# Eight PSUM banks laid out anew, row sums taken from rows without their bias, and a seventh weight slot in a two-layer decoder step

## The chip, the cores and the metric

The kernel runs on one core of a Trainium2 chip. The metric is the device time of one execution in microseconds (us); lower is better. A profiled execution also gives a trace of every instruction on the core's engines: TensorE (PE; PEld is its weight load), VectorE (DVE), ScalarE (ACT), GpSimd (POOL) and SyncE (SP), and of the transfers (DMA).

## The reference

One inference step of a decoder with two layers. Layer 0 mixes tokens by sliding-window attention, layer 1 by gated linear attention; each is followed by a gated FFN with a short convolution, and every sublayer ends in a layer norm. There are 512 prompt rows and 8 sample rows of 1024 features. The change lies in the FFN and in the layer norm ahead of it:

```python
D_MODEL = 1024; SEQ = 512; DEPTH = 2; DEC_BATCH = 8; D_FF = 2816; CONV_W = 3
def conv_ffn(x, buf, w_up, conv_w, conv_b, w_down):
    T = x.shape[1]
    h = x @ w_up
    a, u = h[..., :D_FF], h[..., D_FF:]
    ap = jnp.concatenate([buf.astype(a.dtype), a], axis=1)
    c = conv_b + sum(conv_w[j] * ap[:, j:j + T] for j in range(CONV_W))
    y = (jax.nn.gelu(c, approximate=False) * u) @ w_down
    return y, ap[:, T:]
# in each layer i:
    xp = layer_norm(ALPHA * xp + mp, ln_mix_g[i], ln_mix_b[i])   # mp: the token mixer
    fp, cp = conv_ffn(xp, buf0, ffn_w_up[i], ffn_conv_w[i], ffn_conv_b[i], ffn_w_down[i])
    xp = layer_norm(ALPHA * xp + fp, ln_ffn_g[i], ln_ffn_b[i])
```

The same is done for the sample rows (xs).

## The kernel before

**Numbers.** All operands are float32. Each is split into a high part that TensorE takes whole and a low part, the rest: weights into `wh` and `wl`, rows into `xh` and `xl`. A product is then three matmuls per 128 features: wh·xh, wh·xl and wl·xh. Rows lie transposed (features on the partitions) and in two groups, a with 256 columns and b with 256 and the 8 sample rows.

**Units.** The weights come in *units* of 128 output columns, of 512 KB as a rule. `load_unit` loads a unit on SP's queue into a `raw` tile; ACT makes the high part (L186) and DVE the low part (L192) in one of `WSLOTS` = 6 slots. For some units (`low_by_dma`) the low part is made without DVE: ACT writes the negated high part (L197), and a transfer that POOL issues adds the weights from memory onto it (L198). `run` goes through the units in an order by hand (`order`): a unit's product with group a first, and some units later that with group b; when b is done, the unit's slot is released and the next unit loads (`release`, `load_next`). For the first units of a phase the split is put off (`late`), behind steps of the layer norm that is going on (`parts`).

**The FFN.** There are 22 blocks of 128 gate columns and 128 value columns. Blocks 0 to 3 are *plain*: `ffn_gate` and `ffn_value` each make a `product` into a PSUM bank (`accp`, pool `acc`, four banks); ACT copies the gate out (L764), ACT and DVE do the convolution, ACT the GELU, and DVE multiplies it with the value bank (`hprod`, L785) and splits the result. From block 4 on a block is a *pair* (`ffn_pair`): gate, value and both row groups are made by seven products of half size, with sums of weights and of rows in place of an eighth (Strassen's scheme). One product goes into one bank (`onep`, pool `one`, two banks), six go in twos into tiles of two banks (`widep`, pool `wide`, three tiles). At the first pair the pools of the plain blocks are closed and these take their eight banks. `half_product` writes the matmuls (L292 to L294). The weights of a pair are three slots, made by `pair_tasks`: `upper` (low part by transfer), `lower` and `sums`, and half a slot, `third`. Down products of a finished part of blocks stand between the pairs (`ffn_down2`); those of the last part come at the end (`ffn_down`), the first four (`HEADS`) begun early in `accp` banks and ended when the last block is there.

**Row sums.** The pairs need sums of the two row groups (`th`, `tl`, `t1`). `row_sums` makes them on DVE right after the layer norm. The norm's gain is applied first, its bias only later, by 16 *shifts* on POOL (`shift`, L438: 8 feature blocks, two groups), which stand between the sums, so that each sum finds the bias where it needs it. The sums of the sample rows (`tsum`, L468, L469) need the biased rows; `row_sum1` splits the last sum at the first pair.

**What sets the order.** The code is written in the order of `run`, but a scheduler goes over the program when it is built (`schedule_with_timeline_sim=True`) and sets the order of the instructions on each engine by its own estimate of when each could run; `issue_after` and `keep_in_program_order` bind it in places. On the chip each engine's queue runs in that order. A tile's memory comes from pools, and whatever takes the place of an earlier tile waits for its last reader.

## Time and profile before

| | |
|---|---|
| median of 3 runs | 1149.77 us (1148.25 to 1152.87) |
| the profiled execution's own time | 1149.82 us |
| its span on the core | 1148.1 us |
| PE busy | 1085.6 us, 9174 matmuls |
| DVE busy | 896.0 us |
| ACT busy | 650.6 us |
| POOL busy | 352.7 us |
| mean granted TensorE clock | 0.973 |
| PE waiting for hprod (L785) at the first pair | 15.7 us in two waits, the longer 9.9 |

The span runs from the first to the last instruction on the core, 1.7 us short of the execution's time. Waits are summed by what ended them. In layer 1 of the two (the first) the FFN starts near 175 us and its first pair at 231 us; in the second, near 770 and at 838 us. Times in the trace are counted from the span's start. "Layer 1" and "layer 2" below are these two.

### The profile page before, as it was taken

Reading aid. Unit: us, or ns where it says so; the run is one execution under the profiler, and the core shown is the slowest. Engines: PE = TensorE matmul, PEld = TensorE weight load, DVE = VectorE, ACT = ScalarE, POOL = GpSimd, SP = SyncE. Lnnn points to the kernel's source line nnn. Section 1 sums busy time; section 2 is a strip of 40 time slices with the busy share of each in tenths; the row PEclk is TensorE's granted clock in tenths of the full one; section 3 lists DMA queues with packets and bytes.
Section 4 is the critical chain, followed back from the end, with each engine's and each line's share of the span. In section 5 each row is a group of like instructions: output and inputs, shape, how many; then the busy total and the mean of one; then the engine's idle time right before and its main releaser. Section 6 shows DMA issues by size and latency. Waiting matters only on the chain.

```text
span 1148.1 us, 23839 instructions
## 1 busy us (share of the span) xinstructions
PE 1085.6 (95%) x9174; PEld 1049.6 (91%) x9174; DVE 896.0 (78%) x1784; ACT 650.6 (57%) x1301; POOL 352.7 (31%) x559
## 2 busy tenths in 40 slices
PE   8999997899999999999999999998889999999995
PEld 8897796899999999988899999897789999999985
DVE  7898679758888778868867778789668778777866
ACT  5677555745556665535545556455556665665534
POOL 3575586401111111056311101277411111111045
PEclk9999998989999999999899999998989999999998
DMA  7453023567777777322134454432457777777312
GB/s 235 148 177 97 17 74 102 139 151 179 183 175 177 179 174 181 102 87 92 59 104 138 126 176 157 138 108 95 129 150 180 176 176 182 183 179 179 100 49 75
DMA packets 63601, 158.53 MB, mean 138 GB/s; under 512 B 7896, under 2 KB 28416, under 8 KB 63488
## 3 DMA queue, kind: packets, MB, share of 16 engines
q1 hardware_dynamic: 51536, 119.47, 32.7%
q0 software_dynamic: 9792, 35.66, 18.3%
q10 hardware_dynamic: 2160, 1.89, 0.5%
q8 instruction: 72, 1.18, 0.4%
q14 instruction: 41, 0.34, 0.1%
HBM read 144.32 MB, written 8.47 MB: 133 GB/s over the span
## 4 chain that ended last, share of the span: by engine, by line
PE 63%; DVE 16%; DMA 6%; POOL 5%; ACT 5%; issue 3%; SPq 0%; ACTq 0%; DVEq 0%; POOLq 0%
PE widep L292 8%; PE widep L293 8%; PE widep L294 8%; PE widep L873 5%; PE widep L872 5%; PE widep L871 5%; PE accp L227 4%; PE accp L225 4%; PE accp L229 4%; DMA vb<-dv 2%; PE onep L292 1%; PE onep L294 1%; PE onep L293 1%; DVE wl L192 1%; DMA raw<-in_w_up 1%
## 5 line engine op out<-in xcount | busy, mean ns | idle before, releaser
L297 ACT ACTIVATE wh<-raw 128x1024 fp32r<-128x1024 f32 x72 | 76.4, 1061 | 117.7 <-PE widep L872 84.3
L198 POOL DMA_DIRECT2D wl<-in_w_down x32 | 27.4, 858 | 348.2 <-ACT wl L197 348.2
L186 ACT ACTIVATE wh<-raw 128x1024 fp32r<-128x1024 f32 (+2 forms) x98 | 99.1, 1012 | 59.5 <-PE accp L227 21.6
L293 PE MATMUL widep<-tl,wh 128*128 128x264 f32 (+1 forms) x432 | 119.2, 276 | 0.0
L292 PE MATMUL widep<-th,wh 128*128 128x264 f32 (+1 forms) x432 | 119.2, 276 | 0.0
L294 PE MATMUL widep<-th,wl 128*128 128x264 f32 (+1 forms) x432 | 119.2, 276 | 0.0
L225 PE MATMUL accp<-xs_a,wh 128*128 128x256 f32 x400 | 112.3, 295 | 6.4 <-ACT wh L186 6.0
L225 PE MATMUL accp<-xh_b,wh 128*128 128x264 f32 x400 | 114.4, 286 | 3.1 <-ACT xh_b L423 3.1
L229 PE MATMUL accp<-xh_b,wl 128*128 128x264 f32 x400 | 112.4, 281 | 0.0
L227 PE MATMUL accp<-xl_b,wh 128*128 128x264 f32 x384 | 108.0, 281 | 0.0
L227 PE MATMUL accp<-xs_a,wh 128*128 128x256 f32 x384 | 107.4, 292 | 0.5 <-DVE xs_a L298 0.4
L298 DVE TENSOR_TENSOR wl<-raw,wh 128x1024 fp32r<-128x1024 f32 x72 | 87.9, 1222 | 24.2 <-ACT wh L297 24.2
L192 DVE TENSOR_TENSOR wl<-raw,wh 128x1024 fp32r<-128x1024 f32 (+3 forms) x70 | 82.0, 1178 | 10.6 <-ACT wh L186 9.9
L225 PEld LDWEIGHTS accp<-xs_a,wh 128*128 128x128 f32 x400 | 81.0, 203 | 8.2 <-ACT wh L186 7.0
L809 DVE TENSOR_TENSOR merged<-widep,conv 128x528 f32<-128x528 f32 x72 | 37.4, 560 | 65.4 <-PE widep L294 65.4
L292 PEld LDWEIGHTS widep<-th,wh 128*128 128x128 f32 x432 | 82.3, 190 | 0.0
L294 PEld LDWEIGHTS widep<-th,wl 128*128 128x128 f32 x432 | 82.2, 190 | 0.0
L293 PEld LDWEIGHTS widep<-tl,wh 128*128 128x128 f32 x432 | 82.2, 190 | 0.0
L225 PEld LDWEIGHTS accp<-xh_b,wh 128*128 128x128 f32 x400 | 76.1, 190 | 6.0 <-ACT xh_b L423 3.8
L227 PEld LDWEIGHTS accp<-xs_a,wh 128*128 128x128 f32 x384 | 78.0, 204 | 1.8 <-DVE xs_a L298 1.4
L292 PE MATMUL widep<-xh_b,wh 128*128 128x264 f32 x288 | 79.6, 276 | 0.0
L293 PE MATMUL widep<-xl_b,wh 128*128 128x264 f32 x288 | 79.5, 276 | 0.0
(416 smaller groups left out, 4278.7 us busy)
## 6 DMA issues: line engine op xcount, KB each, us to landing
raw<-in_w_up SPq DMA_DIRECT2D x88, 512.0 KB, 3.6
wl<-in_w_up POOLq DMA_DIRECT2D x36, 512.0 KB, 6.9
raw<-in_w_down SPq DMA_DIRECT2D x32, 512.0 KB, 3.5
wl<-in_w_down POOLq DMA_DIRECT2D x32, 512.0 KB, 6.5
raw<-in_w_gla SPq DMA_DIRECT2D x24, 512.0 KB, 3.5
raw<-in_w_mix_o SPq DMA_DIRECT2D x16, 512.0 KB, 4.3
raw<-in_w_down SPq DMA_DIRECT2D x16, 384.0 KB, 3.1
qs<-hl SPq DMA_DIRECT2D x64, 64.0 KB, 2.2
```

The source lines that it names most:

```text
L186: nc.scalar.activation(h[:, c], r[:, c], AF.Copy)
L192: nc.vector.tensor_tensor(l[:, c], r[:, c], h[:, c].bitcast(F32), op=ALU.subtract)
L225: nc.tensor.matmul(o, h[:, ks], xh, start=k == 0, stop=False)
L227: nc.tensor.matmul(o, h[:, ks], xl, start=False, stop=False)
L229: nc.tensor.matmul(o, l[:, ks], xh, start=False, stop=not tail and k == nt - 1)
L292: self.nc.tensor.matmul(o, h[:, ks], rh, start=k == 0, stop=False)
L293: self.nc.tensor.matmul(o, h[:, ks], rl, start=False, stop=False)
L294: self.nc.tensor.matmul(o, l[:, ks], rh, start=False, stop=k == KD // 2 - 1)
L297: self.nc.scalar.activation(hi, src, AF.Copy)
L298: self.nc.vector.tensor_tensor(lo, src, hi.bitcast(F32), op=ALU.subtract)
L871: nc.tensor.matmul(o, h[:, ks], rh, start=k == 0, stop=False)
L872: nc.tensor.matmul(o, h[:, ks], rl, start=False, stop=False)
```

## The change

There are four edits.

1. *Banks.* `open_wide` opens the pool of single banks ahead of that of two-bank tiles. The single banks are now banks 0 and 1, where the `mps` tiles of the layer norm were; the two-bank tiles are banks 2 to 7.
2. *Row sums.* The sums are taken from rows without the bias, and the bias is added in DVE's own operations (`bias`, and `step`, a difference of biases that POOL makes once). Three DVE operations of 128x1024 become four of 128x256 each. The first subtraction is bound behind `self.rest`, a step of the layer norm, and `row_sums` begins one slot after the norm and not three. All 16 shifts now follow the sums, and `tsum` follows the shifts.
3. *A seventh slot.* When an FFN opens, a slot `extra` is opened for one more unit (pool `wx`), in memory that a conv tile gives up (`nconv_s` shares `sconv`). It takes the seventh unit of the FFN (unit e + 6, where e is its first), is used once and closed; until then a pair's `third` is held back (`half` = 1). The low part of that unit, and of the gate and value units that are loaded without `late`, comes by `low_by_dma`.
4. *Heads.* The four early down products take their banks in the order 2, 3, 0, 1.

```diff
...
         self.psum_cms = cm1, cm0
     def open_wide(self):
-        self.acc, cm0 = self.psum("wide", WIDES)
-        self.one, cm1 = self.psum("one", 2)
+        self.one, cm0 = self.psum("one", 2)
+        self.acc, cm1 = self.psum("wide", WIDES)
         self.psum_cms = cm1, cm0
     def close_psum(self):
...
         if nt == 0:
             return self.load_rank(u)
         r = self.raw.tile([P, KD * P], F32, name="raw")
-        h, l = (self.wts.tile([P, KD * P], F32R, name=name) for name in ("wh", "wl"))
+        h, l = ((self.wx if u == self.extra else self.wts).tile([P, KD * P], F32R, name=name) for name in ("wh", "wl"))
         n = nt * P // pieces
         for c in (slice(i * n, (i + 1) * n) for i in range(pieces)):
             nc.sync.dma_start(out=r[:, c], in_=src[:, c])
             if late:
-                self.spawn(self.parts(u, h[:, c], l[:, c], r[:, c]), 1)
+                self.spawn(self.parts(u, h[:, c], l[:, c], r[:, c], src[:, c]), 1)
                 continue
             if u >= HIACT:
                 nc.scalar.activation(h[:, c], r[:, c], AF.Copy)
             else:
                 nc.gpsimd.tensor_scalar(h[:, c], r[:, c], 1.0, 0.0, op0=ALU.mult, op1=ALU.add)
-            if self.units[u][2] == self.ffn_down2:
+            if self.units[u][2] in (self.ffn_down2, self.ffn_gate, self.ffn_value):
                 self.low_by_dma(l[:, c], h[:, c], src[:, c])
             else:
                 nc.vector.tensor_tensor(l[:, c], r[:, c], h[:, c].bitcast(F32), op=ALU.subtract)
...
         self.nc.scalar.activation(l, h.bitcast(F32), AF.Copy, scale=-1.0)
         self.nc.gpsimd.dma_start(out=l, in_=src, accum_op=ALU.add)
-    def parts(self, u, h, l, r):
+    def parts(self, u, h, l, r, src):
         norm = self.norm if self.norm and self.slot < self.norm[0] else None
...
         n = u - norm[4] if norm else 0
         with behind(norm and (*[norm[1]] * 4, self.square, self.exp)[n]):
             self.nc.scalar.activation(h, r, AF.Copy)
+            if u == self.extra:
+                self.low_by_dma(l, h, src)
+                return
         with behind(norm and (norm[2], *[norm[3]] * 4, self.rest)[n]):
             self.nc.vector.tensor_tensor(l, r, h.bitcast(F32), op=ALU.subtract)
         yield from ()
...
             self.norm = self.slot + HOLD, self.exp, v.ins, xl.ins, self.next_phase() + 1
         if i % 2 == 0:
             if g.i:
-                self.spawn(self.row_sums(i), 3)
+                self.spawn(self.row_sums(i), 1)
             return
         for m in range(KD):
             yield 1 if m else LATEB
...
         nc, half, n = self.nc, KD // 2, P
         a, b = self.groups
-        lo, hi = slice(0, half), slice(half, KD)
+        hi, lo = slice(half, KD), slice(0, half)
         v = nc.vector
-        rows = lambda g, ks: g.x[:, ks, 0:256]
+        bias = lambda m: self.par[:, C_LNB + i * KD + m:C_LNB + i * KD + m + 1]
+        step = self.pp.tile([P, half], F32, name="step")
+        p0 = C_LNB + i * KD
+        nc.gpsimd.tensor_tensor(step, self.par[:, p0 + half:p0 + KD], self.par[:, p0:p0 + half], op=ALU.subtract)
         wide = lambda t: t.rearrange("p (k c) -> p k c", k=half)
         even = lambda t: t.rearrange("p k (j t) -> p k t j", t=2)
+        row = lambda g, k: g.x[:, k, 0:256]
         self.t1 = [self.ln.tile([P, NT - 256], F32, name=name, bufs=c)[:, :256] for name, c in (("sq", 2), ("sq", 2), ("mu", 1), ("msq", 1))]
-        for k in range(half):
-            v.tensor_tensor(self.t1[k], a.x[:, k, 0:256], b.x[:, k, 0:256], op=ALU.subtract)
-            self.shift(b, i, half + k)
+        with self.tc.issue_after(self.rest):
+            v.tensor_tensor(self.t1[0], row(a, 0), row(b, 0), op=ALU.subtract)
+        for k in range(1, half):
+            v.tensor_tensor(self.t1[k], row(a, k), row(b, k), op=ALU.subtract)
         yield 1
         r = wide(self.pp.tile([P, KD * P], F32, name="raw", bufs=2))
         for k in range(half):
-            v.scalar_tensor_tensor(r[:, k], self.t1[k], -1.0, b.x[:, half + k, 0:256], op0=ALU.mult, op1=ALU.subtract)
-            self.shift(a, i, half + k)
-        self.split(self.th[0][:, :, :, :n], self.tl[0][:, :, :, :n], even(r))
-        v.scalar_tensor_tensor(r, r, -1.0, rows(a, hi), op0=ALU.mult, op1=ALU.subtract)
+            v.scalar_tensor_tensor(r[:, k], row(b, half + k), bias(half + k), self.t1[k], op0=ALU.add, op1=ALU.add)
+        th, tl = self.th[0][:, :, :, :n], self.tl[0][:, :, :, :n]
+        nc.scalar.activation(th, even(r), AF.Copy, scale=-1.0)
         for k in range(half):
-            self.shift(b, i, k)
-        yield 1
+            v.scalar_tensor_tensor(tl[:, k], even(r)[:, k], -1.0, th[:, k].bitcast(F32), op0=ALU.mult, op1=ALU.subtract)
+        yield 2
+        for k in range(half):
+            v.scalar_tensor_tensor(r[:, k], r[:, k], bias(half + k), row(a, half + k), op0=ALU.subtract, op1=ALU.subtract)
         self.split(self.th[2], self.tl[2], even(r))
-        v.tensor_tensor(r, rows(b, hi), rows(b, lo), op=ALU.subtract)
+        yield 2
+        for k in range(half):
+            v.scalar_tensor_tensor(r[:, k], row(b, half + k), step[:, k:k + 1], row(b, k), op0=ALU.add, op1=ALU.subtract)
         self.split(self.th[1][:, :, :, :n], self.tl[1][:, :, :, :n], even(r))
+        for m in (*range(half, KD), *range(half)):
+            yield 1
+            for g in (b, a):
+                self.shift(g, i, m)
         ts = self.pp.tile([P, 2, half, NS], F32, name="tsum")
         v.tensor_tensor(ts[:, 0], b.x[:, lo, 256:], b.x[:, hi, 256:], op=ALU.subtract)
         v.tensor_tensor(ts[:, 1], b.x[:, hi, 256:], b.x[:, lo, 256:], op=ALU.subtract)
         for q in range(2):
             self.split(self.th[q][:, :, :, n:], self.tl[q][:, :, :, n:], even(ts[:, q]))
-        yield 1
-        for k in range(half):
-            self.shift(a, i, k)
     def row_sum1(self):
...
         nc.scalar.dma_start(out=self.sconv, in_=self.I["state_conv"][layer])
         self.base = p.tile([P, NF, NS], F32, name="base")
         self.hist = p.tile([P, NF, 2], F32, name="hist")
-        self.nconv_s = p.tile([P, NF, NS, 2], F32, name="nconv_s")
+        self.nconv_s = self.sconv
         self.nconv_p = p.tile([P, NF, 2], F32, name="nconv_p")
         w = lambda j: self.par[:, C_CW + (layer * 3 + j) * NF:C_CW + (layer * 3 + j + 1) * NF].unsqueeze(2).broadcast_to([P, NF, NS])
         b = self.par[:, C_CB + layer * NF:C_CB + (layer + 1) * NF].unsqueeze(2).broadcast_to([P, NF, NS])
...
         end = self.units[u][1] - 1
         if g.i == 0 and m == 0:
-            self.heads = [self.acc.tile([P, 512], F32, name="accp") for _ in range(HEADS)]
+            heads = [self.acc.tile([P, 512], F32, name="accp") for _ in range(HEADS)]
+            self.heads = heads[2:] + heads[:2]
             for i, ps in enumerate(self.heads):
                 self.down_steps(g, u + i, ps, range(end))
         if g.i == 0 and m < HEADS:
...
                 if u == len(self.units):
                     return
                 self.nu += 1
-                late = self.units[u][1] and any(e < u < e + 6 for e in (*self.phases[2:4], *self.phases[5:6]))
+                late = self.units[u][1] and any(e < u < e + 6 + (e != self.phases[3]) for e in (*self.phases[2:4], *self.phases[5:6]))
                 one = [("live", lambda: self.load_unit(u, late=late))]
                 self.todo = self.pair_tasks(u) if self.units[u][2] == self.ffn_pair else one
             kind, f = self.todo[0]
             if kind == "live":
-                if self.live == WSLOTS:
+                if self.more:
+                    self.more, self.extra = False, self.nu - 1
+                elif self.live == WSLOTS:
                     return
-                self.live += 1
+                else:
+                    self.live += 1
             else:
                 if self.half == 1:
                     return
...
         nc = self.nc
         self.plan()
         self.nu = self.live = WSLOTS
-        self.todo, self.half = [], 0
+        self.todo, self.half, self.more, self.extra = [], 0, False, None
         self.attn_open()
         self.later, self.slot, self.seq, self.norm = [], 0, 0, None
         for i, u in self.order():
...
                 self.unit = u
             if i == 0 and pre:
                 pre()
+                if pre != self.gla_open:
+                    self.wx, self.wx_cm = self.open(f"extra{u}")
+                    self.more, self.half = True, 1
+                    self.load_next()
             self.slot += i + 1 if i == 2 else 1
             if i == 2:
                 f(u, *a)
             else:
                 self.resume(f(self.groups[i], u, *a))
-            if i == 1:
+            if i == 1 and u == self.extra:
+                self.close(self.wx_cm)
+                self.half, self.extra = 0, None
+                self.load_next()
+            elif i == 1:
                 self.release()
             self.due()
         while self.later:
```

How the edits stand in the program is shown at three places of the first FFN, as the built programs order them; a row is line, operation, output and inputs, and size, and `x4` counts like instructions in a row. The lines of the program after the change are its own.

POOL, from the layer norm's end to the first pair. Before, the shifts stand in four runs of four between copies of the first plain blocks; the accumulating transfers (L198) come later:

```order
L301 COPY hist<-aext 128x2
L438 TENSOR_SCALAR x_a<-x_a,par 128x256 x4
L438 TENSOR_SCALAR x_b<-x_b,par 128x264 x4
L438 TENSOR_SCALAR x_a<-x_a,par 128x256 x4
L438 TENSOR_SCALAR x_b<-x_b,par 128x264 x4
L761 MEMSET aext 128x2
...
L198 DMA wl<-in_w_up 128x1024
L301 COPY aext<-hist 128x2
L301 COPY nconv_p<-aext 128x2
L301 COPY nconv_s<-aext 128x8
L198 DMA wl<-in_w_down 128x1024
```

After, all 16 stand in one run (8 times the two rows shown in the middle), between the issue for a down unit's low part and that for the low part of a pair's upper weights:

```order
L198 DMA wl<-in_w_up 128x1024
L304 COPY nconv_p<-aext 128x2
L304 COPY sconv<-aext 128x8
L198 DMA wl<-in_w_down 128x1024
L441 TENSOR_SCALAR x_b<-x_b,par 128x264
L441 TENSOR_SCALAR x_a<-x_a,par 128x256
...
L304 COPY aext<-hist 128x2
L198 DMA wl<-in_w_up 128x1024
```

The shifts have moved from ahead of the plain blocks' last products to a place behind one transfer and in front of another; that last one writes `wl_3345`, which is read below.

PE, from the last plain product of group b to the first pair's two-bank tile. Before, the first pair's single-bank product (12 matmuls, `onep_3396`) stands right behind the last plain product, `accp_3332`:

```order
L229 MATMUL accp_3332<-xh_b_89,wl_3091 128x264
L292 MATMUL onep_3396<-xs_a_86,wh_3135 128x256
L293 MATMUL onep_3396<-xs_a_86,wh_3135 128x256
L294 MATMUL onep_3396<-xs_a_86,wl_3136 128x256
...
L292 MATMUL widep_3411<-xs_a_86,wh_3135 128x256
```

After, the first pair's single-bank product (now `onep_3413`) stands earlier, between plain products, and behind the last plain product (`accp_3349`) stands that of the *second* pair, `onep_3606`:

```order
L232 MATMUL accp_3349<-xh_b_89,wl_3020 128x264
L295 MATMUL onep_3606<-xs_a_86,wh_3344 128x256
L296 MATMUL onep_3606<-xs_a_86,wh_3344 128x256
L297 MATMUL onep_3606<-xs_a_86,wl_3345 128x256
...
L295 MATMUL widep_3428<-xs_a_86,wh_3096 128x256
```

So two single-bank products have moved ahead of the first two-bank tile, and the third matmul of the second of them reads `wl_3345`.

DVE, ahead of the last plain block's `hprod`. Before, `tsum` stands some 40 instructions earlier, and these rows come last:

```order
L298 TENSOR_TENSOR xl_b_90<-sq_2848,xh_b_89 128x2x128
L298 TENSOR_TENSOR xl_b_90<-sq_2849,xh_b_89 128x2x128
L298 TENSOR_TENSOR xl_b_90<-mu_2850,xh_b_89 128x2x128
L298 TENSOR_TENSOR xl_b_90<-msq_2851,xh_b_89 128x2x128
L298 TENSOR_TENSOR wl_3365<-raw_3324,wh_3364 128x1024
L785 TENSOR_TENSOR hprod_3357<-conv_3315,accp_3332 128x264
```

After, `tsum`, which waits for the shifts, is among them:

```order
L797 TENSOR_TENSOR hprod_3279<-conv_3244,accp_3254 128x264
L483 TENSOR_TENSOR tsum_3285<-x_b_88 128x32
L484 TENSOR_TENSOR tsum_3285<-x_b_88 128x32
L301 TENSOR_TENSOR xl_b_90<-sq_2794,xh_b_89 128x2x128
...
L780 SCALAR_TENSOR_TENSOR conv_3320<-aext_3317,par_78,conv_3320 128x256
L301 TENSOR_TENSOR wl_3382<-raw_3341,wh_3381 128x1024
L797 TENSOR_TENSOR hprod_3374<-conv_3320,accp_3349 128x264
```

The small sums have moved behind the shifts' new place and into the last stretch of DVE's work ahead of the first two-bank tile. The second layer's FFN has the same order at these places.

## The prediction

> **What bounds the kernel now.** I read the page first: busy shares and the chain that ended last.
>
> ```profile
> PE 1085.6 (95%) x9174; PEld 1049.6 (91%) x9174; DVE 896.0 (78%) x1784; ACT 650.6 (57%) x1301; POOL 352.7 (31%) x559
> PE 63%; DVE 16%; DMA 6%; POOL 5%; ACT 5%; issue 3%; SPq 0%; ACTq 0%; DVEq 0%; POOLq 0%
> ```
>
> TensorE (PE) is busy for 95% of the span, but a busy PE may run slowly, so I went on to stretches. The columns are: from:to, length, busy us and count of PE, PEld, DVE, ACT and POOL, granted TensorE clock, DMA share, GB/s.
>
> ```profile
> 260.00:480.00 220.00, 220.00 (x1964) 220.00 (x1963) 177.39 (x298) 130.33 (x190) 28.37 (x56) 1.00 0.72 169
> 183.00:204.00 21.00, 15.21 (x75) 12.52 (x74) 18.90 (x42) 9.31 (x21) 15.55 (x24) 0.76 0.14 52
> 225.00:231.00 6.00, 0.12 (x2) 0.10 (x1) 5.52 (x12) 4.68 (x11) 1.96 (x4) 0.91 0.69 106
> 231.00:237.00 6.00, 6.00 (x29) 6.00 (x30) 0.43 (x1) 1.43 (x3) 0.13 (x2) 0.52 0.50 143
> 770.00:800.00 30.00, 24.96 (x177) 21.51 (x175) 28.41 (x57) 15.84 (x33) 20.47 (x24) 0.94 0.32 106
> 828.00:838.00 10.00, 0.17 (x1) 0.20 (x2) 8.38 (x18) 6.20 (x13) 1.96 (x4) 0.63 0.62 159
> 838.00:841.00 3.00, 3.00 (x15) 3.00 (x16) 0.43 (x1) 0.34 (x2) 0.13 (x2) 0.52 0.98 283
> ```
>
> In the pair stage (260 to 480) PE never stops: 220 us / 1964 = 0.112 us per matmul at full clock. That stage the change leaves alone. What can move is the start of each FFN, which has two holes. The first (183 to 204; in layer 2 within 770 to 800) leaves PE idle for 21 − 15.2 = 5.8 us and 30 − 25.0 = 5.0 us. The second (225 to 231; 828 to 838) is one wait between the last plain block and the first pair; after it PE runs at a granted clock of 0.52, 6 us / 29 = 0.207 us per matmul, for some 6 us in layer 1 and 3 us in layer 2. The timeline (start, duration, operation, in brackets the idle time before it and its releaser) names both, and the end of the wait on DVE:
>
> ```profile
> 196.99 0.58 PE L225 MATMUL accp<-xs_a,wh 128*128 128x256 f32 x1 [2.24 <-ACT wh L186]
> 230.94 0.55 PE L292 MATMUL onep<-xs_a,wh 128*128 128x256 f32 x1 [5.88 <-DVE hprod L785]
> 837.83 0.55 PE L292 MATMUL onep<-xs_a,wh 128*128 128x256 f32 x1 [9.87 <-DVE hprod L785]
> 230.37 0.42 DVE L785 TENSOR_TENSOR hprod<-conv,accp 128x264 f32<-128x264 f32 x1
> ```
>
> The first pair product cannot start before the last plain block has been read out of its bank by the product with the gate (hprod).
>
> **The change, part by part.** What I price by is the row sums' own work, the weight splits and the shifts of the layer norm's bias on POOL. First the shifts of layer 1 (four in each row), then a small copy on POOL, and the first small sum, which waits for POOL:
>
> ```profile
> 188.37 3.69 POOL L438 TENSOR_SCALAR x_a<-x_a,par 128x256 f32<-128x256 f32 x4 [1.75 <-DVE sq L452]
> 192.84 3.37 POOL L438 TENSOR_SCALAR x_b<-x_b,par 128x264 f32<-128x264 f32 x4 [0.78 <-DVE xl_b L424]
> 196.20 4.55 POOL L438 TENSOR_SCALAR x_a<-x_a,par 128x256 f32<-128x256 f32 x4
> 200.73 2.04 POOL L438 TENSOR_SCALAR x_b<-x_b,par 128x264 f32<-128x264 f32 x4
> 202.88 0.19 POOL L301 COPY nconv_s<-aext 128x8 f32<-128x8 f32 x1
> 202.81 0.19 DVE L468 TENSOR_TENSOR tsum<-x_b 128x32 f32<-128x32 f32 x1 [1.79 <-POOL aext L761]
> ```
>
> Together 3.69 + 3.37 + 4.55 + 2.04 = 13.65 us for 16 shifts, 0.85 each; 1.14 each in the third row, beside busy DVE work, and 0.51 in the last, of which DVE itself waited 1.79 us. Then groups of operations (busy us, mean ns of one) and the accumulating transfers' landing times:
>
> ```profile
> L197 ACT ACTIVATE wl<-wh 128x1024 fp32r<-128x1024 f32 x68 | 71.6, 1053 | 1.1
> L186 ACT ACTIVATE wh<-raw 128x1024 fp32r<-128x1024 f32 x80 | 84.5, 1056 | 50.6 <-PE accp L227 19.5 <-PE widep L293 18.5 <-DMA raw<-in_w_mix_o 9.0
> L764 ACT COPY aext<-accp 128x264 f32<-128x264 f32 x8 | 2.9, 363 | 10.8 <-PE accp L232 10.8
> L192 DVE TENSOR_TENSOR wl<-raw,wh 128x1024 fp32r<-128x1024 f32 x48 | 61.1, 1274 | 10.4 <-ACT wh L186 9.9 <-PE accp L229 0.3
> L198 POOL DMA_DIRECT2D wl<-in_w_up x36 | 31.1, 865 | 54.4 <-ACT wl L197 52.6 <-ACT conv L839 1.6 <-issue 0.2
> DMA to landing us min/median/max: 5.4/6.5/8.9
> L460 DVE SCALAR_TENSOR_TENSOR raw<-raw,x_a 128x1024 f32<-128x1024 f32 x2 | 2.4, 1212 | 0.0
> L465 DVE TENSOR_TENSOR raw<-x_b 128x1024 f32<-128x1024 f32 x2 | 2.4, 1216 | 0.0
> L457 DVE SCALAR_TENSOR_TENSOR raw<-sq,x_b 128x256 f32<-128x256 f32 x4 | 1.9, 514 | 0.0
> q0 software_dynamic: 9792, 35.66, 18.3%
> ```
>
> *Instructions.* In each layer three operations of 128x1024 on DVE (two sums, one low part) become four of 128x256: 3 × (4 × 0.514 − 1.22) = +2.5 us. Three weight low parts go from DVE to the accumulating transfer: DVE −3 × 1.27 = −3.8, ACT +3 × 1.05 = +3.2, POOL +3 × 0.87 = +2.6 us, DMA 3 × 512 KB more. The 68 transfers of q0 took 18.3% of 1148 us, so 3.1 us of all engines each, 9.3 us per layer, against a DMA share of 0.14 in the first hole. I cost all this at nothing by itself: DVE ends 1.3 us better, ACT was idle for half of 183 to 204. If that cover failed, ACT's 3.2 us would stand in the path once per layer.
>
> *Seventh weight slot and single banks in front: the first hole.* In the order the seventh unit's product now stands between the first b products, and 12 matmuls of the first pair are taken between plain blocks, so PE has other work at 197. The whole idle time of the hole can be filled, 5.8 and 5.0 us. Against it stand new waits in PE's order: for the extra unit's transferred low part, for another transferred low part, and twice for a bank that is still being read. The nearest rows are the list of what PE waited for (sum, times, longest):
>
> ```profile
> PE accp L229 <- DVE wl L192: 3.2, 4, 1.4
> PE accp L888 <- DVE merged L809: 3.5, 2, 1.8
> ```
>
> A wait for a low part lasts 3.2 / 4 = 0.8 us, one for a bank 3.5 / 2 = 1.75. I take four at 0.8 = 3.2, since the hoisted matmuls give the bank's reader time. The gain is 2.6 us in layer 1 and 1.8 in layer 2; with four at 1.4 (5.6) it is nothing, with none it is all 5.8 and 5.0.
>
> *Shifts after the sums: the second hole.* Here the change makes a new wait. Before, the shifts lie at 188 to 203 between the sums. Now all 16 stand in one run on POOL's queue, behind the issue of a down unit's accumulating transfer, and behind them stands the issue for the low part of the second pair's weights. PE's order has that pair's 12 single-bank matmuls, the third of which reads this low part, right after the last plain block and ahead of the first two-bank product. So everything on PE waits for: the point X where the plain block's end frees the down unit's slot (PE's last matmul of the group-b product accp_3216, some blocks earlier), ACT's high and low part, the issue, 16 shifts, one copy, the second issue and its landing.
>
> X comes 92 matmuls before the hole: 225.1 − 92 × 0.112 = 214.8 before, so 212.2 after. Add 1.06 + 1.05 for the two ACT parts, 0.36 for ACT's copy that stands ahead of them, 0.87 for the issue, 13.65 for the shifts at their mean of before, 0.19 for the copy on POOL and 6.5 for the landing: 212.2 + 23.7 = 235.9. In layer 2: X at 827.9 − 10.3 = 817.6, less 1.8 is 815.8, and PE goes on at 839.5.
>
> By then 14 matmuls of pairs are done (12 hoisted, and 2 that need the high part alone). Before, the same 14 were done at 230.94 + 14 × 0.207 = 233.8 and 837.83 + 2.8 = 840.6. So layer 1 loses 2.1 us and layer 2 gains 1.1. The clock was by then partly regained before, while after the change the slow stretch begins at this point: 14 × (0.207 − 0.112) = 1.3 us in each layer, 2.7 in all.
>
> The old gate lies beside it: the small sums (tsum) wait for the last low shift of x_b and stand in DVE's queue ahead of the last hprod. Shifts end at 212.2 + 17.0 = 229.2; DVE's whole work in the hole of before is 5.52 us; so hprod is done at some 234.7, and the two-bank product, 10 matmuls later than 235.9, doesn't wait. It is only 1.2 us from being the gate itself.
>
> *A rule weighed.* The prices of the shifts lie between 16 × 0.51 = 8.2 us and 16 × 1.14 = 18.2 us, −5.5 and +4.6 per layer. I take the mean, 13.65, since DVE in 210 to 230 is partly busy as it was in 188 to 203. The Trainium skill, page “GPSIMD Engine Reference”, section Key points, says that GpSimd shares its SBUF interfaces with VectorE and contends with VectorE instructions that have two SBUF inputs. The trace agrees in direction (1.14 beside DVE's sums, 0.51 where DVE waited), and since the DVE operations quoted here from this place (hprod, wl) read two inputs, the rule by itself speaks for 1.14 throughout and a sum of about 1162.6; by the mean row the sum is 1153.5.
>
> *Landing* is 5.4 to 8.9: −1.1 or +2.4 per layer. I take the median.
>
> *Heads of the down product swapped.* The first early product still waits for the last merge of the last pair (the 3.5 us above, once per layer), because in the order it depends on that DVE operation before and after: 0, with a gain of up to 3.5 if banks were freed one at a time, and as much loss if the swapped order waited for a later bank.
>
> *Sum.* +2.1 − 1.1 + 2.7 = +3.7 us on the profiled execution of 1149.82 us (span 1148.1 and 1.7 around it; the median of the runs is 1149.77, the same): 1153.5 us.
>
> **Rivals.**
> *Shifts are quick (faster).* If they run at 0.51 each, the chain is 5.45 us shorter per layer: 1153.5 − 10.9 = 1142.6. For it: DVE no longer makes the sums beside them. Against it: only one of four rows shows it, while DVE stood still.
> *POOL starved (slower).* At 1.14 each, the chain is 4.55 longer per layer: 1153.5 + 9.1 = 1162.6. It decides from a mean of 0.91 on, where the sum passes 1155.5. For it: DVE was busy for 5.52 of the 6 us of the hole, and three rows of four are at 0.84 or above. This is what the page's rule gives.
> *The second hole goes.* If the low part were there in time, PE would pass without a stop: 1149.8 − 5.9 − 9.9, less the slow clock after them (29 × 0.095 + 15 × 0.095 = 4.2) and 4.4 from the first holes: 1125.4. It would need the chain 12 us shorter; against it stand 16 shifts in one queue.
>
> **How the numbers follow.** The main case, 1153.5 with 1147 to 1158 as its own range (first holes filled wholly, −6.4, or not at all, +4.4), has 0.47; quick shifts 0.20; starved POOL 0.26; no second hole 0.07. About ±0.5%, 1144.0 to 1155.5, is what a measurement of this kernel can tell from no change. Of the main case 0.36 lies within and 0.11 above. Faster: 0.20 + 0.07 = 0.27; same 0.36; slower 0.26 + 0.11 = 0.37. The range 1140 to 1164 takes in the quick shifts with some of the first hole's spread and the starved POOL with a little of the landing's, and leaves out the last rival (0.07) and the outer ends of the two others (some 0.1).
>
> **What will show it.** Right: 16 shifts in a row on POOL near 216 to 230 with a mean near 0.85; PE idle from about 224 to 236 and from 827 to 839, ended by the accumulating transfer at the matmul that reads the second pair's low part (L297); no 2.24-us wait near 197; granted clock near 0.5 for some us after each hole. Wrong: that wait is ended by hprod (L797), so the small sums are the gate; or PE stays busy there; or the first hole is as deep as before, with X at 215 or later.

## The result and the profile after

The changed kernel takes 1140.62 us (median of 8 runs, 1136.84 to 1145.35); the kernel before, run beside it, 1149.67 us. The ratio is 0.992, with a 95% interval of 0.9898 to 0.9943: faster by 0.8%. No change or a slightly slower kernel (1153.5 us) was forecast. The time lies at the low end of the range, beside the rival of quick shifts (1142.6), but not for that rival's reason alone.

The profiled execution took 1140.54 us. From its page, engine by engine:

```profile
span 1138.8 us, 23875 instructions
PE 1079.0 (95%) x9174; PEld 1044.8 (92%) x9174; DVE 898.1 (79%) x1796; ACT 655.3 (58%) x1307; POOL 339.0 (30%) x567
```

The same 9174 matmuls keep PE busy for 1079.0 us and not 1085.6. So of the 9.3 us by which the span is shorter (1148.1 to 1138.8), 6.6 us are matmuls that followed each other faster, and only 2.7 us are idle time of PE (62.5 to 59.8).

Where this was gained is read between two places that both kernels pass in each layer: the first product of the FFN and the first early down product, which waits for the last merge in both (columns as in the prediction). First the two layers before, then after:

```profile
166.90:491.40 324.50, 310.35 (x2670) 306.79 (x2668) 259.92 (x452) 190.09 (x293) 68.25 (x118) 0.97 0.65 156
770.30:1096.70 326.40, 308.45 (x2670) 304.24 (x2669) 260.75 (x454) 190.57 (x294) 70.50 (x118) 0.97 0.63 155
```

```profile
168.90:488.20 319.30, 305.37 (x2670) 303.08 (x2668) 258.30 (x459) 191.73 (x295) 63.98 (x120) 0.98 0.66 162
767.00:1087.50 320.50, 306.06 (x2671) 302.56 (x2669) 266.81 (x465) 193.72 (x300) 59.72 (x120) 0.99 0.66 161
```

Layer 1 is 5.2 us shorter, 5.0 of them busy time; layer 2 is 5.9 us shorter, 2.4 of them busy time. Of these 11.1 us, 7.4 are faster matmuls. That is the main reading of this case: the sum of the prediction priced the first hole by its idle time alone. In a second profile of the changed kernel (after_again) the layers are 5.1 us shorter each, with 5.7 and 1.0 us less busy time, so layer 1's reading holds, and layer 2's gain there is mostly idle time. The profiles differ by 9.3 us and not by 11.1, since the changed kernel's began its first FFN 2.0 us later (168.92 and not 166.92): its granted clock in 134 to 140 us, a stage that no edit touches, was 0.72, and 1.00 in the profile before. Two profiles of one program (low_dve below, run twice) differ there in the same way, 0.72 and 1.00, so this is not the change.

The stretches show where in the layers it was gained. The first hole, the stage around it, the second hole and what follows it:

```profile
183.00:204.00 21.00, 18.76 (x155) 17.57 (x153) 20.32 (x52) 15.90 (x30) 5.18 (x13) 1.00 0.45 127
175.00:210.00 35.00, 30.50 (x249) 28.60 (x248) 32.43 (x72) 26.78 (x48) 12.35 (x22) 1.00 0.56 144
221.50:229.00 7.50, 0.08 (x1) 0.00 (x0) 5.17 (x14) 2.91 (x8) 4.56 (x11) 0.72 0.47 79
229.00:237.00 8.00, 7.91 (x45) 7.91 (x46) 1.84 (x3) 1.08 (x2) 0.13 (x2) 0.62 0.15 57
```

The first hole (183 to 204) holds 155 matmuls where it held 75, at a granted clock of 1.00 where it was 0.76. The second hole is still there, and it is what the prediction said it would be. PE's two longest waits in 175 to 245 us (sum, times, longest):

```profile
PE onep L297 <- DMA wl<-in_w_up: 7.5, 1, 7.5
PE accp L228 <- DVE hprod L797: 1.9, 2, 1.8
```

and the two longest in 790 to 850 us:

```profile
PE accp L228 <- DVE hprod L797: 6.8, 3, 4.7
PE onep L297 <- DMA wl<-in_w_up: 1.5, 1, 1.5
```

In layer 1 PE stops at the matmul that reads the second pair's low part, for 7.5 us. In layer 2 it waits for a bank first, 4.7 us at once, and later 1.5 us for the transfer. The timeline of layer 1, with POOL's queue and the two gates (start, duration, operation, idle time before it):

```profile
229.09 0.58 PE L297 MATMUL onep<-xs_a,wl 128*128 128x256 f32 x1 [7.51 <-DMA wl<-in_w_up]
209.88 0.37 ACT L776 COPY aext<-accp 128x264 f32<-128x264 f32 x1
211.50 0.86 POOL L198 DMA_DIRECT2D wl<-in_w_down  x1 [0.19 <-issue]
212.09 0.80 POOL L441 TENSOR_SCALAR x_b<-x_b,par 128x264 f32<-128x264 f32 x1
...
223.27 0.48 POOL L441 TENSOR_SCALAR x_a<-x_a,par 128x256 f32<-128x256 f32 x1
223.70 0.24 POOL L304 COPY aext<-hist 128x2 f32<-128x2 f32 x1
223.87 0.78 POOL L198 DMA_DIRECT2D wl<-in_w_up  x1
223.32 0.46 DVE L483 TENSOR_TENSOR tsum<-x_b 128x32 f32<-128x32 f32 x1 [1.89 <-POOL x_b L441]
227.66 0.42 DVE L797 TENSOR_TENSOR hprod<-conv,accp 128x264 f32<-128x264 f32 x1
```

Point X of the prediction, the end of the group-b product that frees the down unit's slot, is at 209.00: the first row here is that product's last matmul, 92 plain matmuls and the 12 hoisted ones ahead of the hole, and the second is the down unit's high part, which ACT starts as the last reader of the old one ends.

```profile
208.72 0.28 PE L232 MATMUL accp<-xh_b,wl 128*128 128x264 f32 x1
208.92 1.06 ACT L186 ACTIVATE wh<-raw 128x1024 fp32r<-128x1024 f32 x1
```

The 16 shifts run from 212.1 to 223.7, one after the other, and the transfer's issue stands behind them. It lands 5.2 us later (229.09 − 223.87). The last product with the gate ends at 228.08, 1.0 us ahead; 1.2 was forecast.

How much of each layer's gain lies ahead of X is read from the stretches between the FFN's first product and X, first before (with 214.8 and 817.6, the prediction's X of before), then after (in layer 2 X is at 810.1):

```profile
166.90:214.80 47.90, 41.44 (x301) 38.24 (x300) 43.65 (x83) 26.03 (x50) 31.31 (x41) 0.89 0.29 94
770.30:817.60 47.30, 40.74 (x300) 36.90 (x300) 43.88 (x83) 26.78 (x51) 33.05 (x39) 0.93 0.28 93
```

```profile
168.90:209.00 40.10, 36.02 (x298) 34.12 (x296) 37.53 (x79) 27.86 (x51) 15.94 (x26) 1.00 0.49 133
767.00:810.10 43.10, 37.03 (x298) 34.47 (x297) 40.23 (x84) 29.66 (x55) 15.73 (x26) 1.00 0.45 124
```

X comes 7.8 and 4.2 us sooner. Of that, idle time is only 2.4 and 0.5 us; 5.4 and 3.7 us are busy time of nearly the same matmuls (298 and not 301 or 300). The hole of before falls into two parts that show why:

```profile
183.00:192.40 9.40, 5.84 (x33) 4.07 (x31) 9.40 (x24) 5.08 (x12) 4.46 (x8) 1.00 0.15 59
192.40:202.70 10.30, 8.06 (x32) 7.15 (x33) 8.31 (x16) 3.88 (x7) 9.86 (x12) 0.50 0.16 52
```

In the second part PE is busy for 8.06 us at half the clock, which costs some 4 us. In the first the clock is full, but 33 matmuls keep PE busy for 5.84 us, where 33 × 0.112 = 3.7 would do: many start 0.22 us apart (as at 187.73, 187.95 and 188.17) and still count as busy throughout. In after_again, X comes 7.9 and 3.9 us sooner, with 5.9 and 2.5 us less busy time.

One row of layer 2 was in nobody's sum:

```profile
813.81 7.64 DVE L780 SCALAR_TENSOR_TENSOR conv<-aext,par,conv 128x256 f32<-128x256 f32 x1
813.58 0.80 POOL L441 TENSOR_SCALAR x_b<-x_b,par 128x264 f32<-128x264 f32 x1
820.71 0.47 POOL L441 TENSOR_SCALAR x_a<-x_a,par 128x256 f32<-128x256 f32 x1
```

The first and the last of the 16 shifts (the second and third row) frame one step of the convolution on DVE. It took 7.64 us; its like take about 0.47 there. The shifts ran at 0.47 to 0.58 after the first. Here POOL was not starved by DVE but the reverse. The issue of the transfer did not wait for the shifts here: it came at 825.50, 3.73 us after POOL was free, when ACT had made the negated high part.

### The profile page after: what moved, and what is told of

It is laid out like the page before. It is cut to its first block, busy times and chain, and to the rows that moved or that the text cites. A ratio compares the mean times of both kernels' runs of the same rounds, so it can differ in the third digit from the quotient of the medians.

```text
span 1138.8 us, 23875 instructions
## 1 busy us (share of the span) xinstructions
PE 1079.0 (95%) x9174; PEld 1044.8 (92%) x9174; DVE 898.1 (79%) x1796; ACT 655.3 (58%) x1307; POOL 339.0 (30%) x567
## 4 chain that ended last, share of the span: by engine, by line
PE 57%; DVE 12%; DMA 5%; POOL 3%; issue 2%; ACT 2%; SPq 0%; ACTq 0%; DVEq 0%; POOLq 0%
PE widep L295 8%; PE widep L296 8%; PE widep L297 8%; PE widep L885 5%; PE widep L884 5%; PE widep L883 5%; DMA vb<-dv 3%; PE accp L230 3%; PE accp L228 3%; PE accp L232 3%; PE onep L297 1%; PE onep L296 1%; PE onep L295 1%; DVE xs_a L427 1%; POOL x_a L337 1%
## 5 line engine op out<-in xcount | busy, mean ns | idle before, releaser
L198 POOL DMA_DIRECT2D wl<-in_w_down x32 | 27.6, 864 | 338.2 <-ACT wl L197 337.8
L228 PE MATMUL accp<-xs_a,wh 128*128 128x256 f32 x400 | 110.6, 291 | 2.8 <-ACT xs_a L426 1.1
L230 PE MATMUL accp<-xs_a,wh 128*128 128x256 f32 x384 | 105.2, 287 | 0.2
L228 PEld LDWEIGHTS accp<-xs_a,wh 128*128 128x128 f32 x400 | 79.1, 198 | 4.9 <-ACT xs_a L426 1.3
L192 DVE TENSOR_TENSOR wl<-raw,wh 128x1024 fp32r<-128x1024 f32 (+3 forms) x64 | 75.3, 1182 | 7.2 <-ACT wh L186 6.6
L297 PE MATMUL widep<-xh_b,wl 128*128 128x264 f32 x288 | 79.5, 276 | 0.0
```

Source lines behind the costliest of these rows:

```text
L192: nc.vector.tensor_tensor(l[:, c], r[:, c], h[:, c].bitcast(F32), op=ALU.subtract)
L228: nc.tensor.matmul(o, h[:, ks], xh, start=k == 0, stop=False)
L230: nc.tensor.matmul(o, h[:, ks], xl, start=False, stop=False)
L297: self.nc.tensor.matmul(o, l[:, ks], rh, start=False, stop=k == KD // 2 - 1)
```

## The experiments

The first row is the changed kernel and the others are the experiments; the ratios are to the kernel before, run beside each.

| run | what | median us | ratio, interval | PE busy us (one profile) |
|---|---|---|---|---|
| changed kernel | | 1140.62 | 0.992 (0.9898 to 0.9943) | 1079.0 |
| u_slot | without edit 3 | 1145.25 | 0.9962 (0.9949 to 0.9975) | 1083.2 |
| u_rows | without edit 2 | 1142.95 | 0.9944 (0.9927 to 0.9962) | 1077.5 |
| u_banks | without edit 1 | 1143.33 | 0.9947 (0.9927 to 0.9967) | 1080.2 |
| u_heads | without edit 4 | 1138.96 | 0.9909 (0.9892 to 0.9925) | 1077.3 |
| o_slot | before + edit 3 alone | 1140.56 | 0.9927 (0.991 to 0.9943) | 1079.2 |
| o_rows | before + edit 2 alone | 1143.4 | 0.9958 (0.9935 to 0.998) | 1082.2 |
| late_shifts | shifts in the pair stage | 1142.28 | 0.9934 (0.9918 to 0.9951) | 1080.6 |
| low_dve | second pair's low part on DVE | 1141.99 | 0.9926 (0.991 to 0.9942) | 1085.2 |
| late_dve | both of these | 1135.36 | 0.9877 (0.9862 to 0.9892) | 1077.3 |
| late_dve2 | and gate's and value's low parts on DVE | 1135.45 | 0.9865 (0.984 to 0.989) | 1078.0 |
| after_again | the changed kernel once more | 1140.91 | 0.9924 (0.9905 to 0.9943) | 1077.8 |

One more, low_dve_again, was a single execution of 1141.72 us.

**Which edit?** Four runs each undo one edit of the changed kernel, two do one alone (the shared tile `nconv_s` of edit 3 stays in all six). *u_slot* goes back to six slots; the two places that show it best are:

```diff
-        h, l = ((self.wx if u == self.extra else self.wts).tile(...) for name in ("wh", "wl"))
+        h, l = (self.wts.tile(...) for name in ("wh", "wl"))
-            if self.units[u][2] in (self.ffn_down2, self.ffn_gate, self.ffn_value):
+            if self.units[u][2] == self.ffn_down2:
```

> The changed kernel without edit 3: six slots, the gate's and value's low parts on DVE again, the other three edits kept. Theory A (the first hole, idle time and slow clock together, is where the time came from): the hole near 183 to 204 us comes back with a granted clock near 0.76, 5.5 us per layer, and the time goes back to about 1151 us. Theory B (the time came from the second hole, by the single banks and the row sums): the first hole costs little, and the time stays within 3 us of the changed kernel's 1140.6.

Measured: 1145.25 us, between the two theories. The granted clock in 175 to 210 us falls back to 0.90, PE waits 1.9 us per layer for a unit's high part again, and PE is busy for 1083.2 us. The transfer's wait stays. PE's waits in 160 to 250 us:

```profile
PE onep L294 <- DMA wl<-in_w_up: 7.9, 1, 7.9
PE accp L225 <- ACT xh_b L423: 2.0, 2, 1.4
PE accp L225 <- ACT wh L186: 1.9, 1, 1.9
```

*u_rows* puts back the old `row_sums` with its shifts between the sums:

```diff
-                self.spawn(self.row_sums(i), 1)
+                self.spawn(self.row_sums(i), 3)
     def row_sums(self, i):
+        ...   (as before)
```

> The changed kernel with the row sums and shifts of before (shifts in four runs between the sums), the other three edits kept. Theory A (the run of 16 shifts ahead of the transfer is what keeps the second hole open, 7.5 us in layer 1, and 4.7 + 1.5 us in layer 2 with the convolution held up): those waits go, and the time falls below 1140.6, to about 1130. Theory B (unshifted row sums are a gain of their own, since early shifts hold up the sums on DVE): the time rises to 1145 or more.

Measured: 1142.95 us; neither theory's number. The run of shifts is gone, but PE now waits just as long at another transferred low part, that of a plain unit (waits in 160 to 250 us):

```profile
PE accp L232 <- DMA wl<-in_w_up: 7.5, 1, 7.5
PE onep L297 <- DMA wl<-in_w_up: 1.9, 1, 1.9
```

*u_banks* opens the two-bank tiles first again:

```diff
-        self.one, cm0 = self.psum("one", 2)
-        self.acc, cm1 = self.psum("wide", WIDES)
+        self.acc, cm0 = self.psum("wide", WIDES)
+        self.one, cm1 = self.psum("one", 2)
```

> The changed kernel with the banks' order of before (two-bank tiles in front), the other three edits kept. Theory A: the single-bank products of the first two pairs can no longer go ahead of the last plain product's readout, so up to 24 matmuls x 0.112 = 2.7 us per layer fall back behind the hole, and the time is 1142 to 1146. Theory B (the banks are where the time came from): 1149 or more.

Measured: 1143.33 us, as theory A had it, though the interval overlaps that of the changed kernel. The wait is again for the last product with the gate, 9.1 us in layer 1 and 8.6 us in layer 2.

*u_heads* takes back the order of the early down products:

```diff
-            self.heads = heads[2:] + heads[:2]
+            self.heads = heads
```

> The changed kernel with the early down products' banks in the old order, the other edits kept. Theory A (the first early product waits for the last merge of the last pair in either order): PE's wait there stays near 2 us per layer (1.85 and 1.61 before, 1.95 and 1.68 after), and the time stays within 2 us of 1140.6. Theory B (the swap is worth the wait it names, 3.6 us in two): 1144 or more. Beside that its profile shows a second time whether the convolution step on DVE beside 16 shifts takes 7.6 us in layer 2.

Measured: 1138.96 us, and waits of 1.80 and 1.61 us at the same place: the swap changes nothing that can be measured, as the prediction had it. In this profile no convolution step was held up.

*o_slot* is the kernel before with edit 3 alone (the diff of u_slot the other way round):

> The kernel before with edit 3 alone (seventh slot, and low parts of gate and value units by transfer). Theory A (the first hole, idle time and slow clock, is the main gain): a granted clock of 0.95 or more in 175 to 210 us in place of 0.85, and 1140 to 1145 us, some 5 us for each layer. Theory B (the slot needs the new row sums, since the shifts of before hold up POOL's issues and the sums' DVE work the extra product): 1147 to 1151.

Measured: 1140.56 us. The slot with its transferred low parts alone brings all that the whole change brings. The granted clock in 175 to 210 us is 0.96, as theory A had it:

```profile
175.00:210.00 35.00, 25.86 (x209) 24.20 (x208) 30.90 (x63) 24.61 (x45) 25.50 (x34) 0.96 0.43 120
```

But its large hole is another one. The timeline of PE there and at the first pair:

```profile
211.84 0.58 PE L232 MATMUL accp<-xs_a,wl 128*128 128x256 f32 x1 [7.44 <-DMA wl<-in_w_up]
228.94 0.38 PE L295 MATMUL onep<-xs_a,wh 128*128 128x256 f32 x1 [0.98 <-DVE hprod L788]
```

PE waits 7.4 us for a plain unit's low part, and the hole in front of the first pair has shrunk to 1.0 us.

*o_rows* is the kernel before with edit 2 alone:

> The kernel before with edit 2 alone (sums from unshifted rows, the shifts after them). Theory A (edit 2 only moves the shifts from the first hole to the second, where they stand in front of a transfer or hold DVE): the time stays within 4 us of 1149. Theory B (the unshifted sums are worth half of the change): 1145 or less.

Measured: 1143.4 us, 5.7 us less than the kernel before beside it (1149.12): outside theory A's 4 us, inside theory B's bound. The old gate is still in the second hole (waits for hprod of 8.6 and 7.5 us). Edits 2 and 3 are worth 5.7 and 8.5 us alone, and 8 to 9 together with the other two: they do not add up. The changed kernel and these six versions all keep one wait of 7.4 to 9.1 us in layer 1, whatever its releaser. Between the two places of the result section, layer 1 is 4.0 to 6.6 us shorter than before in the profiles with edit 3 (u_rows, u_banks, u_heads, o_slot, the changed kernel) and 0.7 and 1.6 us in those without it (u_slot, o_rows). So layer 1's gain comes with the slot. Layer 2 shows no such split: u_slot is 3.9 us shorter, o_rows 3.3, o_slot 4.3, u_rows 0.8.

**What holds the second hole?** *late_shifts* moves the shifts into the pair stage and takes the sample rows' sums from unshifted rows:

```diff
-        for m in (*range(half, KD), *range(half)):
-            yield 1
-            for g in (b, a):
-                self.shift(g, i, m)
...
-        v.tensor_tensor(ts[:, 0], b.x[:, lo, 256:], b.x[:, hi, 256:], op=ALU.subtract)
-        v.tensor_tensor(ts[:, 1], b.x[:, hi, 256:], b.x[:, lo, 256:], op=ALU.subtract)
+        for k in range(half):
+            v.scalar_tensor_tensor(ts[:, 0, k], b.x[:, k, 256:], step[:, k:k + 1], b.x[:, half + k, 256:], op0=ALU.subtract, op1=ALU.subtract)
+            v.scalar_tensor_tensor(ts[:, 1, k], b.x[:, half + k, 256:], step[:, k:k + 1], b.x[:, k, 256:], op0=ALU.add, op1=ALU.subtract)
...
+        for m in range(KD):
+            yield 3 if m else 14
+            for g in (b, a):
+                self.shift(g, i, m)
```

> The changed kernel with the 16 shifts moved into the pair stage (two at a time, between the accumulating transfers' issues) and the sample rows' small sums taken from unshifted rows too, with the biases' difference added on DVE. The result computed is the same. Theory A (16 shifts in a run cost the 7.5-us wait in layer 1 and the held-up convolution in layer 2): the transfer of the second pair is issued early, layer 1's hole shrinks to some 3 us, which the last product with the gate ends, layer 2's bank wait of 4.7 us goes, and the time falls to about 1130. Theory B (the hole is set by the work on DVE ahead of the last product with the gate, whatever POOL does): the time stays within 2 us of 1140.6.

Measured: 1142.28 us; theory A fell, and B's time came true for another reason. With no shift on POOL's queue the same transfer is still late:

```profile
227.70 0.58 PE L297 MATMUL onep<-xs_a,wl 128*128 128x256 f32 x1 [4.97 <-DMA wl<-in_w_up]
220.18 0.86 POOL L198 DMA_DIRECT2D wl<-in_w_up  x1 [2.76 <-ACT aext L777]
218.82 1.06 ACT L197 ACTIVATE wl<-wh 128x1024 fp32r<-128x1024 f32 x1
```

ACT makes the negated high part only at 218.82 to 219.88, POOL issues at 220.18, and the landing takes 7.5 us. The shifts had stood in front of a chain that was nearly as late without them.

*low_dve* leaves the shifts and lets DVE make that low part, in the changed kernel:

```diff
             nc.scalar.activation(h, r0, AF.Copy)
-            self.low_by_dma(l, h, src0)
+            if self.units[u][3][1] == PAIRED + 1:
+                nc.vector.tensor_tensor(l, r0, h.bitcast(F32), op=ALU.subtract)
+            else:
+                self.low_by_dma(l, h, src0)
```

> The changed kernel with the low part of the second pair's upper weights made by DVE (1.2 us) and not by ACT, POOL's queue and the transfer; the 16 shifts stay where they are. Theory A (POOL's queue ends the second hole, but the last product with the gate stands 1.0 us behind it): the wait for the transfer goes, a wait for that product takes its place at nearly the same end, layer 1 gains 1 to 2 us, and the time is 1137 to 1141. Theory B (the transfer alone holds PE): layer 1's hole closes, 7.5 us and some slow clock, and the time is 1132 or less.

Measured: 1141.99 us (1138.65 to 1148.29), one us beyond theory A. The profiled execution was the slowest, 1148.29 us. PE's waits in 160 to 250 us show none for the transfer. In its place the first two-bank product (`widep`) waits for the last product with the gate, and a plain product (`accp`) waits 4.8 us for a bank that is read late:

```profile
PE accp L228 <- DVE hprod L800: 6.5, 2, 4.8
PE widep L298 <- DVE hprod L800: 3.1, 1, 3.1
```

Behind that bank's wait stands a convolution step held up beside the shifts, as in layer 2 of the changed kernel; here it comes in layer 1 (the row below) and, with 7.61 us, in layer 2:

```profile
211.53 7.62 DVE L783 SCALAR_TENSOR_TENSOR conv<-aext,par,conv 128x256 f32<-128x256 f32 x1
```

*low_dve_again* is the same kernel, profiled once more:

> The changed kernel with the second pair's low part on DVE, once more, for a second profile of the same program. In the first, of 1148.3 us where the median is 1142.0, a convolution step on DVE took 7.6 us beside the 16 shifts in both layers. Theory A (that step is held up in some executions and not in others, and each hold-up costs 4 to 5 us): if this execution is near 1139, no step takes 7.6 us; near 1143, one of the two does. Theory B (the hold-up is in every execution and the time varies for another reason): both steps take 7.6 us whatever the time.

Measured: 1141.72 us. PE's waits in 160 to 250 us, and the same step of layer 1:

```profile
PE widep L298 <- DVE hprod L800: 6.7, 1, 6.7
PE accp L228 <- DVE hprod L800: 1.6, 1, 1.6
```

```profile
209.86 0.82 DVE L783 SCALAR_TENSOR_TENSOR conv<-aext,par,conv 128x256 f32<-128x256 f32 x1
```

In layer 1 the step took 0.82 us; in layer 2 it was held up again, 7.62 us. So the same program has a hold-up in one execution and not in another. The first early down product of layer 1 comes at 490.17 with it and at 485.39 without. But the first FFN product had already come at 168.18 and 166.24, so the hold-up accounts for 2.8 us of these 4.8. Theory A is right that the step comes and goes, and its number for one hold-up, 1143, is 1.3 us above the time; its price of 4 to 5 us each is too high. Of the 6.6 us between the two executions, 1.9 arose ahead of the first FFN.

*after_again* is the changed kernel itself:

> The changed kernel once more, beside the others of this call. Expected 1140.6 within its spread (1136.8 to 1145.4). Theory A (the held-up convolution step comes and goes): the profile shows it in none, one or both layers, and its time is about 1137, 1140.5 or 1145 accordingly. Theory B: one step of 7.6 us in layer 2 again, whatever the time.

Measured: 1140.91 us; its profile, of 1140.71 us, has no held-up step (0.82 us in layer 2), and waits of 8.2 and 7.0 us for the transfer. Layer 2, from its first FFN product to its first early down product, took 321.4 us without the hold-up and 320.5 with it. So in these two profiles of the changed kernel the hold-up costs nothing: it lengthens the wait for a bank (6.8 and not 1.7 us in all) and shortens that for the transfer (1.5 and not 7.0). Theory A's 1137 for an execution without it did not come.

**Both gates.** *late_dve* puts the edits of late_shifts and low_dve together.

> The shifts moved into the pair stage, and the second pair's low part made by DVE. Theory A (two gates stand side by side, POOL's queue with its transfer, and DVE's queue ahead of the last product with the gate; in the run with shifts moved alone that product was done at 225.3 us and the low part at 227.7): with both eased, PE waits some 3 us in layer 1 for the product with the gate, and the time is 1133 to 1138. Theory B (whichever gate is eased, the next weights arrive no earlier, because the transfers and loads share the DMA engines): a wait for weights remains, and the time stays within 2 us of 1141.

Measured: 1135.36 us, all four runs within 1134.96 to 1136.2. The ratio's interval, 0.9862 to 0.9892, lies below that of the changed kernel and below 1: this version beats both. What is left in front of the first two-bank product:

```profile
226.11 0.49 PE L298 MATMUL widep<-xs_a,wh 128*128 128x256 f32 x1 [2.42 <-DVE hprod L801]
```

and the stretch behind it, with 49 matmuls at a granted clock of 0.87, where the changed kernel had 45 in 8 us at 0.62:

```profile
228.00:234.00 6.00, 6.00 (x49) 6.00 (x49) 2.43 (x3) 2.21 (x4) 0.00 (x0) 0.87 0.36 119
```

*late_dve2* also puts the low parts of gate and value units back on DVE (the second edit of u_slot).

> As the run with shifts in the pair stage and the second pair's low part on DVE, and besides the low parts of the gate and value units (three per layer) back on DVE; seventh slot, banks and heads stay. Theory A (a plain product's wait for a transferred low part, 1.8 us in layer 1 and 4.3 us in layer 2 in that run, is the next gate): these waits go, and the time falls from 1135.4 to about 1130. Theory B (DVE, busy for 20.5 of 21 us in the first hole, becomes the gate with 3 x 1.2 us more per layer): 1135 to 1140.

Measured: 1135.45 us, no change from late_dve: the transfers' waits at plain units go (1.8 and 4.3 us), and the wait for hprod grows from 2.4 to 4.7 us in layer 1 and from 2.1 to 4.0 us in layer 2. DVE is then the gate, as theory B had it, though no run tried this apart.

## Why the prediction was wrong, point by point

- *The step that failed: the price of the first hole.* It was put at the idle time, 5.8 and 5.0 us, less four new waits: 2.6 and 1.8 us. The idle time was about right in layer 1 (2.4 us ahead of X) and too high in layer 2 (0.5). But the quoted row had 75 matmuls in 15.21 us and a granted clock of 0.76 beside the idle time, and the sum put that at nothing. A hole is paid twice, in idle time and in slow matmuls, and an edit that fills it is paid back twice: 5.4 and 3.7 us here. So X came 7.8 and 4.2 us sooner after the FFN's start, and not 2.6 and 1.8. Half of the 8.06 us at half clock, 4 us, is the clock's share in layer 1; much of the rest is that matmuls no longer start 0.22 us apart.
- *The chain behind it was right in kind and 3.6 us too long in layer 1.* From X to PE 23.7 us were forecast and 20.1 measured (209.00 to 229.09): 2.5 us to the first issue, as forecast; 0.6 us and not 0.87 for the issue; 11.7 us and not 13.65 for the shifts (0.73 each); 5.2 us and not 6.5 for the landing. The shifts were inside their bounds, the landing just under its own (5.4), and all fell on the same side. With X 5.2 us ahead of the forecast (for an FFN that began 2.0 us later), layer 1 gained 5.2 us where the sum had a loss of 2.1 + 1.3.
- *Layer 2* was to gain 1.1 us less 1.3; it gained 5.9, and in after_again 5.1. X explains 2.4 us of the difference. Behind X the chain was another one: the shifts took 7.6 us in the profiled execution with the held-up step, near the low bound of 8.2, and 9.0 without it, and in neither did they set the issue of the transfer. POOL waited for ACT's negated high part with the held-up step (3.73 us), and without it ACT had waited 5.29 us for the weights themselves to load.
- *What was right:* the run of 16 shifts on POOL in front of the transfer, its place as the releaser of PE's wait in layer 1, the second gate 1.0 us beside it, a granted clock of 0.62 after the hole, and nothing from the swapped heads. The slow clock after the second hole was right for layer 1 (45 matmuls in 8 us), but the slow clock that goes with the first hole was not set against it. In layer 2 of the profiled execution it was shorter: the granted clock is 0.83 in 820 to 830 us and 0.97 in 825 to 835.
- *The rivals.* Quick shifts came in layer 2 (7.6 us for 16), and that rival's 1142.6 is only 2.0 us above the time. That is luck: late_shifts, which takes all shifts away from there, is no faster than the changed kernel, so the shifts' price did not decide the time. Starved POOL did not come in the changed kernel: single shifts took up to 1.53 us in layer 1, but the mean was 0.73. It did come in u_slot, where the 16 shifts of layer 1 run from 204.41 to 222.53 us, 1.13 each. The rule of the Trainium skill, page “GPSIMD Engine Reference”, section Key points, that the two engines contend for SBUF interfaces agrees with the trace, but in the other direction from the one that I drew from it: it was DVE that stood, 7.6 us for a step of 0.5. The step reads `aext` and `conv`, two inputs in SBUF; of the two operations that the prediction named for the rule, hprod does not fit it, since its second input, `accp`, is a PSUM bank. The chance of a quite closed second hole (0.07) was fair: it is open in every version run.

Not settled: why edits 2 and 3 shorten the starts by 5.7 and 8.5 us alone and by no more than 9 together. That one long wait stays in layer 1 of these versions is shown; that the order of ACT's work (high parts and negated high parts) sets it was only seen in late_shifts and in layer 2 of the changed kernel, and not tried apart.

## What to carry to other kernels

Price a hole in TensorE's work by its idle time and by the pace of the matmuls in and after it: PE's busy time for the same number of matmuls tells how much of a gain is pace, and the granted clock of that stretch how much of this is clock. Compare two profiles between places that both kernels pass, since they can differ by 2 us ahead of the change. Where three or four chains end within a few us of each other, easing one moves the wait to the next; list the ends of all of them, and ease two at a time, as late_dve did. An engine's queue is a chain of its own: look what stands between a transfer's issue and the work it feeds, and also how late that issue would be without it.

## What the runs showed of the hardware

A run of 16 GpSimd operations of 0.47 us each, back to back, can hold up a single VectorE operation for the whole run: 7.64, 7.62, 7.61 and 7.62 us for a step that otherwise takes 0.47 to 0.82. In all four cases the step starts 0.2 us after the first of the 16 and ends 0.3 us after the last. It came in some executions and not in others of the same program. In other executions the step took 0.82 us, and single shifts of the changed kernel up to 1.57 us: there the two engines seem to have taken turns. Kernels with the shifts two at a time (late_shifts, late_dve, late_dve2) showed no such step.
